# Two value products per block and group, with high and low parts in one stationary tile, and moved start, gate and store work, in a two-layer decoder kernel

## The chip, the cores and the metric

The kernel runs on one core of a Trainium2 chip. A core has TensorE (matrix products; PE in the profile, with PEld for its weight loads), VectorE (DVE), ScalarE (ACT), GpSimd (POOL) and SyncE (SP), which issues most DMAs. Each engine works through its own instructions in order. Products are summed in PSUM banks of 128 partitions by 512 float32 columns. The metric is the device time of one execution in microseconds; lower is better.

## The reference

Two layers of a hybrid decoder trunk, 1024 positions, width 1024, all in float32. Cut to what matters here:

```python
for l in range(DEPTH):
    mod = silu(c) @ ada_w[l] + ada_b[l]            # six shifts, scales, gates
    h = rms_norm(x, g_pre_mix[l]) * (1 + scale_m) + shift_m
    q, k, v, u = split(h @ w_in[l] + b_in[l])      # 8 query heads, 2 key/value heads of 64
    q, k = partial_rotary(q, positions), partial_rotary(k, positions)
    attn = sliding_window_attention_with_sinks(q, k, v, sinks[l])   # window and block 128
    pool = causal_pool_mixer(u, pool_w[l], pool_scale[l])
    mix = concat([attn, pool]) @ w_out[l]
    x = x + gate_m * rms_norm(mix, g_post_mix[l])
    h = rms_norm(x, g_pre_ffn[l]) * (1 + scale_f) + shift_f
    f = (silu(h @ w_gate[l]) * (h @ w_up[l])) @ w_down[l]
    x = x + gate_f * rms_norm(f, g_post_ffn[l])
```

## The kernel before

Every float32 operand of a product is split into a high part (a copy rounded to float32r, on ScalarE) and a low part (the rest, a subtraction on VectorE); `split` does both. A product of two such operands is three products on TensorE, `mm3`: high by high, high by low, low by high.

The 1024 positions are two halves of 512, each four blocks of 128. A layer has a mixing stage and a channel stage. In the mixing stage, `q_pass`, `kv_pass` and `u_pass` multiply by `w_in`, attention and pooling run beside them, and `mix_out` multiplies by `w_out`. The channel stage (`up_firsts`, `up_pair`, `down`) multiplies by `w_gate`, `w_up` and `w_down` with sums of quarters, fewer products than the plain form.

In the mixing stage TensorE's order is the order in which the code issues (`tc.manual_schedule`). `weave` runs a dense chain of products and steps side chains in between: a step that yields a gap is due again once so many units have been issued. A unit, `STEP`, is 12 products of 512 columns. The constants `LEADS` (attention), `GAPS`, `CLOSE`, and the numbers handed to `ada_flow`, `attention` and `pool_mix` are such gaps. On the other engines a scheduler orders by readiness and priority.

Attention runs in groups, one for each block and key/value head `n` (four query heads): 32 groups in all. A group turns keys and queries, forms scores (`att_scores`), exponentials (`att_softmax`), turns the probabilities (`att_probs`), and multiplies by values (`att_values`). Sequence block 0 of each layer has one part of values; each other block has two, `vz` (its own values) and `dz` (the step from the block before), with the probabilities masked for the second. So there are 60 pairs of group and part. The values of the two heads lie in a tile of three fields, with 64 columns of zeros between them that GpSimd writes (`att_vals`, L948); group 0 takes the first two fields and group 1 the last two, so that both sum into one PSUM tile `pv`, each filling half of the partitions with zeros:

```python
vh, vl = (v[:, n : n + 2].rearrange("p a d -> p (a d)") for v in vals)
ins = mm3(pv, vh, vl, *probs, opening, closing, None if opening else attn["open"])
```

The bank opens with group 0 and closes with group 1, and then one ScalarE copy (L1075) takes it to `cat`.

`pv` has one PSUM bank. `part` hands out halves of rings of wide tiles, `raw` (2), `hi` (3) and `lo` (3); weights, keys and queries share `hi`, and weights and pooled values share `lo`. `weight_once` loads a weight tile, splits it, and for some keys stores both parts to DRAM (`parted`), from where the second half reads them back into a whole tile of the ring `lo` (L247): in layer 0 those of `u`, in layer 1 all.

The start: SyncE loads `c`, the rows of biases and norms, and the first columns of `ada_w`; ScalarE's queue loads `x`; VectorE works out the rotary angles. The end: for the last half's tiles, `ended` squares and sums a product tile on ScalarE, multiplies it by the gate row G on VectorE (L1778), and `finish` scales, adds the residual and stores.

Of the kernel before, what the change touches and what calls it, by code (L numbers as in the profile page):

```python
# [68 lines left out]
def hybrid_decoder_kernel(  # L69
# [39 lines left out]
        mix=dict(cfa=2, cfb=2, qkv=5, bqkv=1, uT=4, pt=2, vz=4, dz=2, qT=1, pth=4, pwh=1, pwl=1),  # L109
# [41 lines left out]
    nc.gpsimd.dma_start(pos_i, positions[0].rearrange("(t p) -> p t", p=P))  # L151
# [27 lines left out]
    nc.sync.dma_start(c_raw, c[0].rearrange("(p j) -> p j", j=KD))  # L179
    x0 = []  # L180
    for t in range(NT):
        x0.append(t_("fn", [P, D]))
        nc.scalar.dma_start(x0[t], x[0, t * P : (t + 1) * P, :])
# [10 lines left out]
    def rotary_angles():  # L194
        nc.vector.tensor_copy(pos_f, pos_i)
        for i in range(RH):
            nc.vector.tensor_scalar(ang[:, :, i], pos_f, float(inv_freq[i]), None, op0=ALU.mult)
        nc.vector.tensor_scalar(turns, ang, 1.0 / (2.0 * math.pi), None, op0=ALU.mult)
        nc.vector.tensor_scalar(turns, turns, ROUND_MAGIC, None, op0=ALU.add)
        nc.vector.tensor_scalar(turns, turns, ROUND_MAGIC, None, op0=ALU.subtract)  # L200
# [4 lines left out]
        nc.vector.tensor_scalar(up, ang, math.pi, -math.pi, op0=ALU.min, op1=ALU.max)
        nc.vector.tensor_scalar(sin_t[:, :, halves[0]], up, -1.0, None, op0=ALU.mult)
        nc.vector.tensor_tensor(turns, sin_t[:, :, halves[0]], up, op=ALU.max)
        for half in halves:
            nc.vector.tensor_scalar(cos_t[:, :, half], turns, -1.0, math.pi / 2.0, op0=ALU.mult, op1=ALU.add)
# [320 lines left out]
    def ada_gate(l, sub):  # L530
# [3 lines left out]
        def close(half, hi, lo):  # L534
# [9 lines left out]
            nc.vector.tensor_add(gb, bank[0:1, :], gb)  # L544
# [213 lines left out]
    def finish(h, t, fn, ss, G, xt=None, ahead=None):  # L758
# [6 lines left out]
        for i in range(2):  # L765
# [5 lines left out]
            else:  # L771
                nc.vector.scalar_tensor_tensor(
                    fn[t][:, cs], fn[t][:, cs], rstd, xt[:, cs], op0=ALU.mult, op1=ALU.add
                )
# [290 lines left out]
    def att_values(n, vals, probs, opening, closing, cat, t):  # L1065
# [8 lines left out]
        if closing:
            nc.scalar.activation(  # L1075
# [768 lines left out]
```

## Time and profile before

| what | value |
| --- | --- |
| median of 3 runs | 1867.78 us (1867.1 to 1868.0) |
| the profiled execution | 1870.79 us |
| its span on the core | 1869.1 us |
| granted TensorE clock, mean | 0.997 |
| mean DMA rate over the span | 195 GB/s |

The page gives busy time by engine, then the span in 40 slices of 46.7 us (busy tenths), and the costliest groups:

```profile
PE   7999999999999999999999999999999999999998
DVE  7899885688888978879778788856878888877687
ACT  4885785562222223445648559755522222244452
DMA  9646744665456556844586676446646456574343
```

A group's line names the line of the program, the engine, what is written and read, the count, and after the bar the busy time and the mean of one. An idle time of an engine that is not the bound costs nothing. Start times in a timeline count from the start of the span.

### The profile page before, as it was taken

What the parts mean: (1) busy time and instruction counts of PE and PEld (TensorE: products, weight loads), DVE (VectorE), ACT (ScalarE), POOL (GpSimd) and SP (SyncE); (2) the same over time, 40 slices, a digit from 0 to 9 for tenths busy, and PEclk for the clock granted to TensorE, in tenths of its full rate; (3) what the DMA queues carried; (4) which work ended last, traced back from release to release, by engine and by line L of the source; (5) the groups of instructions that cost most, each with busy time, mean ns of one, the idle gap of its engine ahead of it and who ended that gap; (6) DMA issues with size and microseconds to landing.
All of it is one profiled execution on the core that took longest, in us unless ns stands there. A gap on an engine that the chain in (4) does not pass through costs nothing.

```text
span 1869.1 us, 25361 instructions
## 1 busy us (share of the span) xinstructions
PE 1835.1 (98%) x8662; PEld 1515.4 (81%) x8662; DVE 1501.5 (80%) x2492; ACT 919.7 (49%) x1757; POOL 100.3 (5%) x204
## 2 busy tenths in 40 slices
PE   7999999999999999999999999999999999999998
PEld 5888888888888888888887788888887887888886
DVE  7899885688888978879778788856878888877687
ACT  4885785562222223445648559755522222244452
POOL 0021130000000000000001202200000000000000
PEclk9999999999999999999999999999999999999999
DMA  9646744665456556844586676446646456574343
GB/s 341 201 141 215 259 147 143 208 215 181 167 188 218 183 180 225 298 147 133 194 302 202 213 233 217 155 135 209 220 157 207 162 200 229 176 270 142 113 146 114
DMA packets 237089, 363.84 MB, mean 195 GB/s; under 512 B 17912, under 2 KB 126344, under 8 KB 236960
## 3 DMA queue, kind: packets, MB, share of 16 engines
q1 hardware_dynamic: 236352, 360.13, 57.2%
q10 hardware_dynamic: 576, 2.10, 0.3%
q8 instruction: 68, 1.11, 0.2%
q14 instruction: 61, 0.50, 0.1%
q0 software_dynamic: 32, 0.00, 0.0%
HBM read 274.59 MB, written 87.57 MB: 194 GB/s over the span
## 4 chain that ended last, share of the span: by engine, by line
PE 83%; DVE 8%; DMA 4%; ACT 3%; issue 1%; SPq 1%; DVEq 0%; POOL 0%; ACTq 0%; POOLq 0%
PE acc L285 75%; PE msc L285 3%; PE msc L290 2%; PE pv L285 2%; DVE lo L224 1%; DMA raw<-in_w_up_dram 1%; DMA raw<-in_w_in_dram 1%; ACT hi L223 1%; DVE fn L1322 1%; SPq L426 0%; DVE ada L581 0%; DMA ar<-x 0%; DVE st L1026 0%; ACT sb L1034 0%; DVE raw L1337 0%
## 5 line engine op out<-in xcount | busy, mean ns | idle before, releaser
L223 ACT ACTIVATE hi<-raw 128x1024 fp32r<-128x1024 f32 (+2 forms) x360 | 315.6, 889 | 385.2 <-PE acc L285 243.6
L224 DVE TENSOR_TENSOR lo<-raw,hi 128x1024 fp32r<-128x1024 f32 (+2 forms) x360 | 363.0, 1016 | 115.9 <-ACT hi L223 110.7
L285 PE MATMUL acc<-t,hi 128*128 128x512 f32 x1408 | 432.1, 390 | 3.2 <-ACT hi L223 3.2
L285 PEld LDWEIGHTS acc<-t,hi 128*128 128x128 f32 x1408 | 263.6, 188 | 59.7 <-ACT hi L223 5.6
L285 PE MATMUL acc<-t,lo 128*128 128x512 f32 x704 | 271.9, 389 | 0.8 <-DVE lo L224 0.8
L285 PE MATMUL acc<-hT,hi 128*128 128x512 f32 x832 | 260.2, 394 | 0.0
L285 PE MATMUL acc<-hT,lo 128*128 128x512 f32 x608 | 213.4, 393 | 0.5 <-DVE lo L224 0.4
L285 PE MATMUL acc<-bh,hi 128*128 128x512 f32 x520 | 202.8, 390 | 0.0
L285 PE MATMUL acc<-bh,lo 128*128 128x512 f32 x520 | 202.4, 389 | 0.0
L1322 DVE TENSOR_TENSOR fn<-acc,fn 128x512 f32<-128x512 f32 x220 | 150.8, 686 | 33.7 <-PE acc L285 33.6
L285 PEld LDWEIGHTS acc<-hT,hi 128*128 128x128 f32 x832 | 151.8, 188 | 28.1
L285 PEld LDWEIGHTS acc<-t,lo 128*128 128x128 f32 x704 | 132.1, 188 | 30.0 <-DVE lo L224 2.4
L285 PEld LDWEIGHTS acc<-hT,lo 128*128 128x128 f32 x608 | 112.4, 188 | 25.8 <-DVE lo L224 1.3
L285 PE MATMUL acc<-ph,hi 128*128 128x512 f32 x328 | 126.5, 390 | 0.0
L1247 ACT ACTIVATE fn<-fn 128x512 f32<-128x512 f32 x44 | 27.9, 633 | 188.2 <-DVE fn L1322 188.2
L285 PEld LDWEIGHTS acc<-bh,lo 128*128 128x128 f32 x520 | 97.6, 188 | 20.4
L285 PEld LDWEIGHTS acc<-bh,hi 128*128 128x128 f32 x520 | 97.6, 188 | 20.2
L285 PE MATMUL acc<-b,hi 128*128 128x512 f32 x352 | 108.4, 389 | 0.0
L285 PE MATMUL acc<-lo,hT 128*128 128x512 f32 (+1 forms) x352 | 95.8, 349 | 3.9 <-DMA lo<-parted 2.9
L223 ACT ACTIVATE bh<-two_b 128x512 fp32r<-128x512 f32 x100 | 62.3, 623 | 71.2 <-PE acc L285 70.5
L285 PE MATMUL acc<-hi,hT 128*128 128x512 f32 (+1 forms) x320 | 88.8, 351 | 0.6 <-ACT hT L223 0.5
L285 PE MATMUL acc<-hi 128*128 128x512 f32 x224 | 87.6, 391 | 0.8 <-DVE fn L806 0.8
(320 smaller groups left out, 3235.3 us busy)
## 6 DMA issues: line engine op xcount, KB each, us to landing
raw<-in_w_gate_dram SPq DMA_DIRECT2D x44, 512.0 KB
raw<-in_w_up_dram SPq DMA_DIRECT2D x44, 512.0 KB
cfb<-in_ada_w_dram SPq DMA_DIRECT2D x80, 256.0 KB
raw<-keeps SPq DMA_DIRECT2D x40, 512.0 KB
keeps<-fn SPq DMA_DIRECT2D x66, 256.0 KB
ar<-in_ada_w_dram SPq DMA_DIRECT2D x64, 256.0 KB
two_b<-in_w_down_dram SPq DMA_DIRECT2D x30, 512.0 KB
lo<-parted SPq DMA_DIRECT2D x28, 512.0 KB
```

What stands on the lines that cost most here:

```text
L223: a = nc.scalar.activation(hi, src, AF.Copy)
L224: v = nc.vector.tensor_sub(lo, src, hi.bitcast(F32))
L285: return nc.tensor.matmul(dst, lhs, rhs, start=start, stop=stop)
L290: return nc.tensor.transpose(dst, src, eye_)
L1247: nc.scalar.activation(g, g, AF.Silu)
L1322: nc.vector.tensor_add(halves_of(dst)[m], bank, halves_of(src)[m])
```

## The change

The edits, by place:

- Values: `att_vals` writes one tile with high and low part of each head side by side (64 + 64 columns). `att_values` multiplies it by the high and by the low probabilities, two products. High rows land in partitions 0 to 63 of `pv`, low rows in 64 to 127. Each group opens and closes the bank itself; a ScalarE copy brings the low half to `cat` and a VectorE add puts the high half on top. The tiles `vz` and `dz` are half as many.
- Start: `x` and `c` come over SyncE's queue, ahead of the rows (now in a tile `ada`) and of `ada_w`; positions over ScalarE's. The rotary angles are worked out on GpSimd, the cosines later on VectorE. The first row of `ada_w` products is issued before the turn of the rows.
- `weight_once`: six more tiles (`EARLY`) of layer 0 are stored, over GpSimd's queue, and read back for the second half in place of being loaded and split again. Reads take the rings `lo` and `hi` in turn.
- Gate row: ScalarE copies the bank, and GpSimd adds and multiplies in place of VectorE.
- End: the product with G of the last tiles goes to another tile.
- Gaps: `CLOSE`, `GAPS`, `LEADS` and others have new values.

```diff
-    nc.sync.dma_start(c_raw, c[0].rearrange("(p j) -> p j", j=KD))
-    x0 = []
+    x0 = [t_("fn", [P, D]) for _ in range(NT)]
     for t in range(NT):
-        x0.append(t_("fn", [P, D]))
-        nc.scalar.dma_start(x0[t], x[0, t * P : (t + 1) * P, :])
+        nc.sync.dma_start(x0[t], x[0, t * P : (t + 1) * P, :])
+        if t == 0:
+            nc.sync.dma_start(c_raw, c[0].rearrange("(p j) -> p j", j=KD))
...
     def rotary_angles():
-        nc.vector.tensor_copy(pos_f, pos_i)
+        nc.gpsimd.tensor_copy(pos_f, pos_i)
...
+    acc = ada_first_row(wss[0])
     par = layer_cols(0, rows0)
-    acc = ada_first_row(wss[0])
...
     parted = {}
+    EARLY = ("q4_0", "q5_0", "q6_0", "q7_0", "kv4_0", "kv6_0")
...
         if key in parted:
-            both = part("lo", 1024)
+            recent["ring"] = "hi" if recent.get("ring") == "lo" else "lo"
+            both = part(recent["ring"], 1024)
...
-        if key[0] == "u" or key[-1] == "1":
+        early = key in EARLY
+        if early or key[0] == "u" or key[-1] == "1":
...
-                nc.sync.dma_start(both[:, i * 512 : (i + 1) * 512], src.bitcast(F32))
+                (nc.gpsimd if early else nc.sync).dma_start(both[:, i * 512 : (i + 1) * 512], src.bitcast(F32))
...
-            nc.vector.tensor_add(gb, bank[0:1, :], gb)
-            nc.vector.tensor_mul(gb, gb, gg)
+            gr = t_("ph", [P, 512], F32R)[0:1].bitcast(F32)
+            nc.scalar.activation(gr, bank[0:1, :], AF.Copy)
+            nc.gpsimd.tensor_add(gb, gr, gb)
+            nc.gpsimd.tensor_mul(gb, gb, gg)
...
-        vh = t_(tag, [P, 3, HD], F32R)
-        vl = t_(tag, [P, 3, HD], F32R)
-        for v in (vh, vl):
-            nc.gpsimd.tensor_copy(v[:, 1, :], picks[:, 0:1].bitcast(F32).to_broadcast([P, HD]))
+        both = t_(tag, [P, NKV, 2, HD], F32R)
         vsrc = src.rearrange("p (n d) -> p n d", d=HD)
-        nc.scalar.activation(vh[:, 0:3:2, :], vsrc, AF.Copy)
-        nc.vector.tensor_sub(vl[:, 0:3:2, :], vsrc, vh[:, 0:3:2, :].bitcast(F32))
-        return vh, vl
+        nc.scalar.activation(both[:, :, 0, :], vsrc, AF.Copy)
+        nc.vector.tensor_sub(both[:, :, 1, :], vsrc, both[:, :, 0, :].bitcast(F32))
+        return both
...
-        vh, vl = (v[:, n : n + 2].rearrange("p a d -> p (a d)") for v in vals)
-        ins = mm3(pv, vh, vl, *probs, opening, closing, None if opening else attn["open"])
-        if opening:
-            attn["open"] = ins
+        both = vals[:, n].rearrange("p o d -> p (o d)")
+        mm(pv, both, probs[0], opening, False)
+        mm(pv, both, probs[1], False, closing)
         if closing:
-            nc.scalar.activation(
-                cat[:, :, t * P : (t + 1) * P], pv.rearrange("p (j q) -> p j q", j=GRP), AF.Copy
-            )
+            high, low = (pv[o * HD : (o + 1) * HD].rearrange("p (j q) -> p j q", j=GRP) for o in range(2))
+            dst = cat[n * HD : (n + 1) * HD, :, t * P : (t + 1) * P]
+            nc.scalar.activation(dst, low, AF.Copy)
+            nc.vector.tensor_add(dst, high, dst)
...
-                att_values(n, vals, prob, n + i == 0, n == NKV - 1 and i == len(parts) - 1, cat, t)
+                att_values(n, vals, prob, i == 0, i == len(parts) - 1, cat, t)
...
-    LEADS = (0.9, 0.85, 0.21, 2.72, 1.2, 0.94)
+    LEADS = (0.9, 0.9, 0.25, 2.72, 1.2, 0.75)
...
-                nc.vector.tensor_mul(fn[1][t][:, 0:512], fn[1][t][:, 0:512], G[:, 0:512])
-                finish(1, t, fn[1], ss[1], G, tail[t], aheads[t])
+                nc.vector.tensor_mul(fn[0][t][:, 0:512], fn[1][t][:, 0:512], G[:, 0:512])
+                finish(1, t, (fn[0][t], fn[1][t]), ss[1], G, tail[t], aheads[t])
```

TensorE's order in the first half's attention, at the second block's first group (its second value part, `pv<-pth,dz`) and the second group's first part (`pv<-pth,vz`); `acc` are products of `q_pass` and `u_pass`, `msc<-sa,qT` scores. Before:

```order
L285 MATMUL pv<-pth,dz 128x512 x3
L285 MATMUL msc<-sa,qT 128x256 x4
L285 MATMUL acc<-hi,hT 128x512
L285 MATMUL acc<-lo,hT 128x512
L285 MATMUL acc<-hi,hT 128x512
L285 MATMUL msc<-sa,qT 128x256 x4
L285 MATMUL acc<-hi,hT 128x512
L285 MATMUL acc<-lo,hT 128x512
L285 MATMUL acc<-hi,hT 128x512 x2
L285 MATMUL acc<-lo,hT 128x512
L285 MATMUL acc<-hi,hT 128x512
L285 MATMUL pv<-pth,vz 128x512 x3
```

And of the change:

```order
L292 MATMUL pv<-pth,dz 128x512 x2
L292 MATMUL acc<-hi,hT 128x512
L292 MATMUL acc<-lo,hT 128x512
L292 MATMUL acc<-hi,hT 128x512
L292 MATMUL msc<-sa,qT 128x256 x4
L292 MATMUL acc<-lo,hT 128x512 x3
L292 MATMUL pv<-pth,vz 128x512 x2
```

The value steps have two products in place of three, and one of the two score steps has moved ahead of the first of them.

SyncE's order in layer 1, while the second half's parted weights are read (`lo<-parted`, `hi<-parted`), between loads of `ada_w` (`cfb`) and the gate's rows (`ar`, `gate`). Before:

```order
L247 DMA lo<-parted 128x1024 x2
L546 DMA gate<-ar 1x512
L539 DMA ar<-in_ada_b_dram 1x512
L247 DMA lo<-parted 128x1024
L568 DMA cfb<-in_ada_w_dram 128x512 x5
L247 DMA lo<-parted 128x1024
```

And of the change:

```order
L253 DMA hi<-parted 128x1024
L253 DMA lo<-parted 128x1024
L577 DMA cfb<-in_ada_w_dram 128x512 x2
L555 DMA gate<-ar 1x512
L577 DMA cfb<-in_ada_w_dram 128x512 x2
L253 DMA hi<-parted 128x1024
L253 DMA lo<-parted 128x1024
```

The reads go to two rings in turn, and the store of the gate row stands between loads of `ada_w`.

ScalarE's order at the start: splits of weights (`hi<-raw`), the row of `ada_w` (`ar<-msc`), the first normalised pieces (`uT<-msc`) and their split (`hT<-uT`). Before:

```order
L223 ACTIVATE hi<-raw 128x512 x2
L450 ACTIVATE ar<-msc 1x256
L223 ACTIVATE hi<-raw 128x512
L667 ACTIVATE uT<-msc,colp 128x512
L223 ACTIVATE hT<-uT 128x512
```

And of the change:

```order
L227 ACTIVATE hi<-raw 128x512 x2
L457 ACTIVATE ar<-msc 1x256
L676 ACTIVATE uT<-msc,colp 128x512
L227 ACTIVATE hi<-raw 128x512
L227 ACTIVATE hT<-uT 128x512
```

The piece `uT` has moved ahead of the third split of a weight.

More of the change, by code (lines that the diff above doesn't have):

```diff
@@ L108, in hybrid_decoder_kernel @@
     REGIONS = dict(
-        mix=dict(cfa=2, cfb=2, qkv=5, bqkv=1, uT=4, pt=2, vz=4, dz=2, qT=1, pth=4, pwh=1, pwl=1),
+        mix=dict(cfa=2, cfb=2, qkv=5, bqkv=1, uT=4, pt=2, vz=2, dz=1, qT=1, pth=4, pwh=1, pwl=1),
         up=dict(t2=8, t1=8, t3=8, b22=8, t4=8),
@@ L150, in hybrid_decoder_kernel @@
     pos_i = const.tile([P, NB], I32, name="pos_i")
-    nc.gpsimd.dma_start(pos_i, positions[0].rearrange("(t p) -> p t", p=P))
+    nc.scalar.dma_start(pos_i, positions[0].rearrange("(t p) -> p t", p=P))
     ones_r = const.tile([P, 1], F32R, name="ones_r")
@@ L194, in rotary_angles @@
     def rotary_angles():
-        nc.vector.tensor_copy(pos_f, pos_i)
+        nc.gpsimd.tensor_copy(pos_f, pos_i)
         for i in range(RH):
[L197 to L200, printed above, removed]
+            nc.gpsimd.tensor_scalar(ang[:, :, i], pos_f, float(inv_freq[i]), None, op0=ALU.mult)
+        nc.gpsimd.tensor_scalar(turns, ang, 1.0 / (2.0 * math.pi), None, op0=ALU.mult)
+        nc.gpsimd.tensor_scalar(turns, turns, ROUND_MAGIC, None, op0=ALU.add)
+        nc.gpsimd.tensor_scalar(turns, turns, ROUND_MAGIC, None, op0=ALU.subtract)
         for part in two_pi_parts():
-            nc.vector.scalar_tensor_tensor(ang, turns, -part, ang, op0=ALU.mult, op1=ALU.add)
+            nc.gpsimd.tensor_scalar(cos_t[:, :, 0:RH], turns, -part, None, op0=ALU.mult)
+            nc.gpsimd.tensor_add(ang, cos_t[:, :, 0:RH], ang)
         halves = [slice(0, RH), slice(RH, ROT)]
         up = sin_t[:, :, halves[1]]
[L205 to L209, printed above, removed]
+        nc.gpsimd.tensor_scalar(up, ang, math.pi, -math.pi, op0=ALU.min, op1=ALU.max)
+        nc.gpsimd.tensor_scalar(sin_t[:, :, halves[0]], up, -1.0, None, op0=ALU.mult)
         for g, w in enumerate(WINDOWS):
@@ L212, in rotary_angles, with rotary_cosines @@
         nc.vector.reciprocal(rcnt, rcnt)
+    def rotary_cosines():
+        halves = [sin_t[:, :, 0:RH], sin_t[:, :, RH:ROT]]
+        after(nc.vector.tensor_tensor(turns, *halves, op=ALU.max), recent["split"])
+        for half in (slice(0, RH), slice(RH, ROT)):
+            nc.vector.tensor_scalar(cos_t[:, :, half], turns, -1.0, math.pi / 2.0, op0=ALU.mult, op1=ALU.add)
     def rotary_tables(prev):
@@ L387, in hybrid_decoder_kernel, with load_col_rows @@
     NROW = 6 * KD + 2 * KD + 4 + 4
-    def load_col_rows(l):
-        rows = t_("ar", [P, 512])[:NROW, :P]
+    def load_col_rows(l, tag="ar"):
+        rows = t_(tag, [P, 512])[:NROW, :P]
         r = 0
@@ L772, in finish @@
                 nc.vector.scalar_tensor_tensor(
-                    fn[t][:, cs], fn[t][:, cs], rstd, xt[:, cs], op0=ALU.mult, op1=ALU.add
+                    fn[1][:, cs], fn[i][:, cs], rstd, xt[:, cs], op0=ALU.mult, op1=ALU.add
                 )
-            nc.sync.dma_start(out[0, h * T + rows.start : h * T + rows.stop, cs], fn[t][:, cs])
+            nc.sync.dma_start(out[0, h * T + rows.start : h * T + rows.stop, cs], (fn[t] if xt is None else fn[1])[:, cs])
     def natural_proj(fn, left, wsrc, ss, G, last, free):
@@ L1167, in pool_mix @@
             late = (g, hi, lo_)
-            yield 1.7 if h else 2.82
+            yield 2.37 if h else 2.81
         mapped(*late)
@@ L1639, in gate_flow @@
             one, two = ada_gate(l, 0)
-            yield from ada_flow([one], [cats[0][1][:, i, :] for i in range(4)], 2.25)
+            yield from ada_flow([one], [cats[0][1][:, i, :] for i in range(4)], 2.39)
             while 1 not in cats:
                 yield 0.5
-            yield from ada_flow([two], [cats[1][1][:, i, :] for i in range(4)], 1.91)
+            yield from ada_flow([two], [cats[1][1][:, i, :] for i in range(4)], 2.49)
         gate = Chain(gate_flow())
-        att = attention(0, qkvs[0], par["sink"], cats[0][0], 0.47, 3.23)
+        att = attention(0, qkvs[0], par["sink"], cats[0][0], 0.55, 3.23)
         def dense():
@@ L1660, in hybrid_decoder_kernel @@
         late = att
-        att = attention(1, qkvs[1], par["sink"], cats[1][0], 14.0, 3.95)
+        att = attention(1, qkvs[1], par["sink"], cats[1][0], 11.6, 3.95)
         ring = [cats[1][1][:, i, :] for i in range(4)]
-        pair = Chain(ada_flow(ada_pair(l, 1, par["cols"], par["abf"]), ring, 0.91))
+        pair = Chain(ada_flow(ada_pair(l, 1, par["cols"], par["abf"]), ring, 0.77))
         weave(out0, late, att, pair)
```

12 lines of the change are left out of this document (7 added, 5 removed).

## The prediction

> **What bounds the kernel now.** First the page: busy time by engine, then the chain that ended last.
>
> ```profile
> PE 1835.1 (98%) x8662; PEld 1515.4 (81%) x8662; DVE 1501.5 (80%) x2492; ACT 919.7 (49%) x1757; POOL 100.3 (5%) x204
> PE 83%; DVE 8%; DMA 4%; ACT 3%; issue 1%; SPq 1%; DVEq 0%; POOL 0%; ACTq 0%; POOLq 0%
> ```
>
> TensorE is busy for 98% of the span and 83% of the chain lies on it. So a product that disappears is worth its issue time, unless the engine then waits. The issue time is not the mean of 390 ns in the groups (that is start to end, and neighbours overlap); it is read from an unbroken piece of the chain, and the value products show the same pace (three, then the next instruction):
>
> ```profile
> 515.85 85.11 PE acc L285 x375
> 116.22 0.84 PE L285 MATMUL pv<-pth,vz 128*128 128x512 f32 x3
> 116.90 0.39 PE L285 MATMUL acc<-hi,hT 128*128 128x512 f32 x1
> ```
>
> 85.11 / 375 = 0.227 us for one product of 512 columns, and 116.90 - 116.22 = 0.68 us for three. Next, where TensorE waits (microseconds in total, times, longest):
>
> ```profile
> PE msc L402 <- DVE ident L156: 11.8, 1, 11.8
> PE acc L285 <- ACT hi L223: 3.2, 4, 1.4
> PE acc L285 <- DMA lo<-parted: 2.9, 2, 1.6
> PE msc L285 <- ACT qT L999: 2.5, 3, 0.9
> ```
>
> One wait at the start, and small ones. The kernel is bound by TensorE, with a head, a tail and a few short waits around it.
>
> **Values: 60 products less.** The product count and the eviction of before:
>
> ```profile
> L285 PE MATMUL pv<-pth,vz x96: 387/389/632, 86.3 to 1213.4; 128*128 128x512 f32 x96
> L285 PE MATMUL pv<-pth,dz x84: 387/389/478, 112.4 to 1216.8; 128*128 128x512 f32 x84
> L1075 ACT ACTIVATE cfa<-pv x8: 578/582/642, 97.7 to 1079.7; 128x512 f32<-128x512 f32 x8
> L224 DVE TENSOR_TENSOR pth<-msc,pth x32: 671/680/692, 84.4 to 1211.0; 128x512 fp32r<-128x512 f32 x32
> ```
>
> 96 + 84 = 180 products, three for each of 60 (block, group) pairs; two stay, so 60 go: 60 x 0.227 = **-13.6 us**. Weight loads overlap (PEld is its own row), so the wider stationary tile costs nothing.
>
> What is added: each of the 32 head groups gets its own eviction, a ScalarE copy of one half and a VectorE add of the other, where 16 ScalarE copies did before. A 64-partition form is not in the trace; the nearest rows are 0.582 us (PSUM copy of 512 columns) and 0.680 us (PSUM operand, 512 columns), bounds 0 and those. I take the whole 0.58 and 0.68. That is +9.3 us of ScalarE (16 more) and +21.8 us of VectorE, beside TensorE as long as those engines have room:
>
> ```profile
> 60.00:160.00 100.00, 98.00 (x573) 83.36 (x572) 92.42 (x207) 77.14 (x201) 25.81 (x44) 1.00 0.54 173
> 160.00:320.00 160.00, 159.25 (x790) 131.33 (x789) 126.82 (x245) 114.78 (x269) 22.92 (x43) 1.00 0.59 198
> 100.00:120.00 20.00, 20.00 (x112) 16.71 (x111) 19.71 (x45) 16.47 (x46) 5.83 (x9) 1.00 0.48 150
> 120.00:140.00 20.00, 18.97 (x107) 15.94 (x106) 19.76 (x44) 16.05 (x45) 5.91 (x11) 1.00 0.46 145
> L544 DVE TENSOR_TENSOR ar<-msc,ar x8: 666/671/673, 107.0 to 1550.7; 1x512 f32<-1x512 f32 x8
> ```
>
> Columns: stretch, length, then busy PE, PEld, DVE, ACT, POOL. Layer 0's first attention half (60 to 160) is the tight one: VectorE 92.4 of 100 us, and 39.5 of 40 between 100 and 140. There it gains 8 adds (+5.4), and loses four gate operations of 0.67 (-2.7, now on ScalarE and GpSimd) and, as the second half reads ready-made high and low parts of six weight tiles, six splits of 0.68 (-4.1). Net -1.4, but not in the same microseconds: **+1.0 us** (0 to +3.2, the 14 products that this half saves).
>
> **A new wait: the pv bank.** It is one bank. Before, both groups of a block added into it; now the second group opens it afresh and must wait for copy and add of the first. The tightest place is the second block's first group closing and its second opening, whose rows of TensorE's order stand in the part on the change.
>
> Now six products of 512 and four of 256 columns stand between the two value steps; four of 256 columns pass in 1037.54 - 1037.07 = 0.47 us (below), so that is 6 x 0.227 + 0.47 = 1.83 us. In the third block the same count gives 2.55 us, elsewhere 3.9 to 13. What an eviction takes to finish is seen at a late one of before:
>
> ```profile
> 1034.85 0.84 PE L285 MATMUL pv<-pth,dz 128*128 128x512 f32 x3
> 1037.32 0.58 ACT L1075 ACTIVATE cfa<-pv 128x512 f32<-128x512 f32 x1
> 1037.07 0.63 PE L285 MATMUL msc<-sa,qT 128*128 128x256 f32 x4
> 1037.54 0.60 PE L290 MATMUL msc<-ident,sb 128*128 128x128 f32 x4
> ```
>
> It ended 1037.90 - 1035.69 = 2.2 us after the product; without a queue it is 0.6. With the add, 1.4 to 2.9 us, plus 0.16 of the product's own tail. The wait is 0 to 1.3 us at the first place and 0 to 0.6 at the second, for each layer; TensorE runs in order, so everything behind waits too. I take 0.8 a layer: **+1.6 us** (0 to +3.8).
>
> **Reads of ready-made parts.** In layer 1 the second half's weights come back from DRAM:
>
> ```profile
> 1037.89 3.02 PE L285 MATMUL acc<-lo,hT 128*128 128x512 f32 x12
> 1042.23 0.98 PE L285 MATMUL acc<-lo,hT 128*128 128x512 f32 x3 [1.32 <-DMA lo<-parted]
> 1044.78 1.65 PE L285 MATMUL acc<-lo,hT 128*128 128x512 f32 x3 [1.57 <-DMA lo<-parted]
> 1040.94 0.34 SPq L247 DMA_DIRECT2D lo<-parted  x1
> SPq L247 <- PE acc L285: 14.1, 4, 7.6
> 1044.00:1051.00 7.00, 6.22 (x20) 5.07 (x21) 2.23 (x6) 3.56 (x8) 0.00 (x0) 0.51 0.46 131
> ```
>
> The read is issued at 1040.94, just as TensorE's twelve products end: its buffer of the ring lo came free only then. Two waits, 2.9 us, and then 7 us at a granted clock of 0.51 in place of 1.00: 7 x 0.49 = 3.4 us more.
>
> In SyncE's order of now (the part on the change has its rows) the rings hi and lo take turns, so a read has about twice the time to land. It still stands behind loads that wait for VectorE. I take **-5.0 us** of the 6.3 (0 to -6.3).
>
> The stores behind those parts: six of layer 0's tiles are now written out too, by twelve DMAs on GpSimd's queue.
>
> ```profile
> 1.35 1.04 POOL L151 DMA_DIRECT2D pos_i<-in_positions_dram  x1 [0.34 <-issue]
> ```
>
> That is 12 x 1.04 = 12.5 us of GpSimd, which is busy 25.8 of the 100 us from 60 on (and the padding copies of the values go), so I cost it at nothing; were GpSimd's masks late by one store, 1.04 us each.
>
> The Trainium skill (TensorE: Matmul & The Clock Gate, "What's actually happening") lets the clock fall to half only after an idle window of about 3.4 us. The trace disagrees: waits of 1.32 and 1.57 us with products between were followed by 0.51. By the rule the half clock would have another cause, the waits' going would bring back 2.9 at most, and with 2.3 of it in place of 5.0 the sum would be 2.7 less.
>
> **Tail.**
>
> ```profile
> 1859.81 1.42 DVE L772 SCALAR_TENSOR_TENSOR sb<-sb,rs,hT 128x512 f32<-128x512 f32 x2
> 1860.11 0.39 PE L285 MATMUL acc<-two_b,lo 128*128 128x512 f32 x1
> 1861.14 0.68 DVE L1417 TENSOR_TENSOR sb<-acc,sb 128x512 f32<-128x512 f32 x1
> 1862.67 0.69 DVE L1778 TENSOR_TENSOR sb<-sb,G 128x512 f32<-128x512 f32 x1 [0.85 <-ACT junk L614]
> 1863.28 0.15 DVE L750 SCALAR_TENSOR_TENSOR rs<-ss,st 128x1 f32<-128x1 f32 x1
> ```
>
> The gate product L1778 writes over what ScalarE is squaring and waits for it; into another tile it runs beside the squaring. Its 1863.28 - 1862.67 = 0.6 us leaves the last chain; the chain of the tile before it shortens alike, so L1417 starts at the last product's end (1860.50) and not at 1861.14. **-1.2 us** (-0.6 to -1.3).
>
> **Head.**
>
> ```profile
> 0.80 6.51 ACTq L183 DMA_DIRECT2D fn<-in_x_dram  x4
> 12.14 5.86 PE L448 MATMUL msc<-cfa,c_act 128*1 128x256 f32 x16
> 18.12 8.42 DMA raw<-in_w_in_dram
> 26.56 0.30 ACT hi L223
> 27.10 0.77 ACT uT L667
> 28.58 3.09 PE acc L285 x12
> ```
>
> The rotary angles leave VectorE for GpSimd, so the identity and the 11.8 us wait go. x now stands ahead of the weights on SyncE and no longer takes ScalarE 6.51 us to issue; the row of L448 can start when its first weights are there, 10 to 12 us by the 6.51 us and the weights' own issues behind it, in place of 12.14. But what is late next is a weight load that lands at 26.54 whatever TensorE did, and ScalarE's split of it ahead of the hT that frees 28.58. ScalarE's new order (its rows stand in the part on the change) puts uT, 0.77 us, before that split. One more table load on ScalarE stands ahead of the first x, where it has nothing else to do. So not 2 us but **-1.2 us** (0 to -2.5). The moved leads I set at 0 (+2.5 to -2.5, the size of the qT wait).
>
> **Sum.** -13.6 + 1.0 + 1.6 - 5.0 - 1.2 - 1.2 = -18.4. The profiled execution took 1870.8 us (span 1869.1 and 1.7 around it), so it would be 1852.4; it lies 3.0 above the median of 1867.8, which gives **1849.4 us**.
>
> **Rivals.**
> 1. *The reads stay late* (0.20). Six tiles of layer 0 now come as 512 KB and not 256 KB; SyncE issues in order, so the wait of layer 1 may stay or appear in layer 0 too. Against it: two rings. Price 2.9 + 3.4 = 6.3: 1855.7.
> 2. *All waits go* (0.10): no pv wait, the whole 6.3, the qT waits of 2.5 too: 1849.4 - 1.6 - 1.0 - 1.3 - 2.5 = 1843.0.
> 3. *The products were cover* (0.08): TensorE waits for evictions in place of computing, and the 13.6 are lost: 1863.0. It speaks for it that VectorE is at 98.7% from 100 to 140; against it that this holds in 40 us only.
> 4. *VectorE becomes the bound of the mixing stages* (0.04), slower: its net work there (+21.8, less 8 gate operations 5.4 and splits 4.1: +12.3) comes onto the path, and only head and tail gain: 1867.8 + 12.3 - 2.4 = 1877.7. It decides once VectorE is full over a whole stage; the rows say 92% and 79%.
> 5. *The half clock is not the waits'* (0.03): then only waits go, 2.3 of the 2.9, and the time is 1849.4 + 2.7 = 1852.1.
>
> **How the numbers follow.** Forecast 0.55 (own range 1845 to 1854). The range 1841 to 1859 takes in rivals 1, 2 and 5 and the bounds of the unknown waits, and leaves out rivals 3 and 4 and some 0.05 below. A measurement tells about 0.2% (3.7 us) from no change: faster 0.55 + 0.20 + 0.10 + 0.03 of rival 5 + 0.03 of rival 3 = 0.91, same 0.05, slower 0.04.
>
> **What would show it.** Right: 120 value products; TensorE's wait list without lo<-parted and with a pv wait on the new add below 4 us in all; granted clock 1.00 all through both mixing stages; the last product some 7.4 us before the end of the span and not 8.6. Wrong: a long list of pv waits, VectorE without gaps from 60 to 160, a second stretch of half clock, or a first 512-column product later than before.

## The result, and the profile after

| | changed kernel | before, same batch |
| --- | --- | --- |
| median | 1890.2 us (1888.9 to 1891.6, 4 runs) | 1867.9 us (1867.1 to 1868.6, 4 runs) |
| ratio | 1.0119, 95% interval 1.0103 to 1.0135 | |
| span of the profiled execution | 1889.8 us | 1869.1 us |
| granted clock, mean | 0.995 | 0.997 |

The change made the kernel slower by 22 us, where 18.4 us less were forecast. The page of the changed kernel, busy time by engine:

```profile
PE 1831.2 (97%) x8602; PEld 1504.6 (80%) x8602; DVE 1507.5 (80%) x2481; ACT 934.5 (49%) x1776; POOL 120.6 (6%) x199
```

60 products are gone (8662 before), and TensorE's busy share fell from 98 to 97% of a longer span: it issues less and waits more. Three of its waits now (us in total, times, longest), and below them a row of the kernel before that the prediction did not show:

```profile
PE msc L455 <- DMA cfa<-in_ada_w_dram: 11.6, 1, 11.6
PE acc L292 <- DVE lo L228: 10.6, 7, 2.5
PE pv L292 <- DVE cfa L1083: 2.7, 1, 2.7
```

```profile
PE acc L285 <- DVE lo L224: 2.2, 4, 1.0
```

Lines of the changed kernel lie four to nine further down (L228 is L224, L292 is L285, L815 is L806). The list no longer has lo<-parted, as forecast, but waits for split weights (`lo`) rose from 2.2 to 10.6 us. Where they lie, the stretches show (stretch, length, then busy PE, PEld, DVE, ACT, POOL, granted clock, DMA share, GB/s); first before, then the changed kernel:

```profile
480.00:640.00 160.00, 159.33 (x701) 130.41 (x700) 140.23 (x182) 43.04 (x50) 0.00 (x0) 1.00 0.57 200
1060.00:1240.00 180.00, 179.23 (x923) 149.14 (x922) 142.95 (x278) 124.92 (x300) 29.08 (x54) 1.00 0.60 196
```

```profile
60.00:160.00 100.00, 94.62 (x553) 79.19 (x552) 90.51 (x200) 77.17 (x198) 21.19 (x35) 1.00 0.55 185
160.00:320.00 160.00, 155.03 (x766) 126.37 (x765) 132.89 (x260) 117.01 (x275) 21.05 (x33) 1.00 0.61 204
480.00:640.00 160.00, 154.82 (x671) 125.86 (x671) 133.43 (x172) 41.90 (x49) 6.71 (x4) 0.99 0.52 178
1060.00:1240.00 180.00, 173.49 (x905) 143.45 (x905) 152.36 (x303) 131.09 (x317) 31.77 (x45) 0.99 0.61 198
```

TensorE is idle 5.4, 5.0, 5.2 and 6.5 us there, against 2.0, 0.8, 0.7 and 0.8 before. Two things are to be seen. From 480 to 640 lies the channel stage, which has no attention and no values: all that the change touched there is the gate row, and VectorE is emptier than before (133 against 140 us) while TensorE waits for it. And in the first attention half (60 to 160) TensorE waits although VectorE, at 90.5 of 100, is no fuller than before (92.4); in the two other mixing stretches VectorE is busier (132.9 against 126.8 us, 152.4 against 143.0), but not full.

The tail did what was forecast: the last product ends at 1882.4, 7.4 us before the end of the span.

```profile
1881.98 0.39 PE L292 MATMUL acc<-two_b,lo 128*128 128x512 f32 x1
1882.41 0.69 DVE L1423 TENSOR_TENSOR sb<-acc,sb 128x512 f32<-128x512 f32 x1
1883.13 0.69 DVE L1786 TENSOR_TENSOR fn<-sb,G 128x512 f32<-128x512 f32 x1
```

L1423 starts as the last product ends, and the gate product L1786 no longer stands behind ScalarE's squaring.

### The profile page after: what moved, and what is told of

It is laid out like the page before. It is cut to its first block, busy times and chain, and to the rows that moved or that the text cites. A ratio compares the mean times of both kernels' runs of the same rounds, so it can differ in the third digit from the quotient of the medians.

```text
span 1889.8 us, 25275 instructions
## 1 busy us (share of the span) xinstructions
PE 1831.2 (97%) x8602; PEld 1504.6 (80%) x8602; DVE 1507.5 (80%) x2481; ACT 934.5 (49%) x1776; POOL 120.6 (6%) x199
## 4 chain that ended last, share of the span: by engine, by line
PE 67%; DVE 15%; DMA 8%; ACT 6%; issue 3%; SPq 0%; POOL 0%; DVEq 0%; POOLq 0%; ACTq 0%
PE acc L292 61%; PE msc L292 3%; DVE lo L228 2%; DMA raw<-in_w_up_dram 2%; PE msc L297 2%; ACT hi L227 1%; DVE fn L1328 1%; DVE ada L590 1%; DMA raw<-in_w_in_dram 1%; DMA ar<-x 1%; DMA cfb<-in_ada_w_dram 1%; PE pv L292 1%; ACT sb L1040 1%; DVE raw L1343 1%; DVE raw L1344 1%
## 5 line engine op out<-in xcount | busy, mean ns | idle before, releaser
L227 ACT ACTIVATE hi<-raw 128x1024 fp32r<-128x1024 f32 (+2 forms) x354 | 311.3, 892 | 388.2 <-PE acc L292 217.8
L228 DVE TENSOR_TENSOR lo<-raw,hi 128x1024 fp32r<-128x1024 f32 (+2 forms) x354 | 359.6, 1022 | 120.8 <-ACT hi L227 114.4
L292 PE MATMUL acc<-t,hi 128*128 128x512 f32 x1408 | 434.1, 391 | 4.5 <-ACT hi L227 4.4
L292 PEld LDWEIGHTS acc<-t,hi 128*128 128x128 f32 x1408 | 264.9, 189 | 62.6 <-ACT hi L227 8.0
L292 PE MATMUL acc<-hT,hi 128*128 128x512 f32 x928 | 287.3, 395 | 0.0
L292 PE MATMUL acc<-t,lo 128*128 128x512 f32 x704 | 273.4, 392 | 9.6 <-DVE lo L228 9.6
L292 PE MATMUL acc<-bh,hi 128*128 128x512 f32 x520 | 202.9, 390 | 1.2 <-ACT sb L1426 1.2
L292 PE MATMUL acc<-bh,lo 128*128 128x512 f32 x520 | 202.4, 389 | 0.0
L292 PEld LDWEIGHTS acc<-hT,hi 128*128 128x128 f32 x928 | 168.7, 188 | 31.0
L292 PE MATMUL acc<-hT,lo 128*128 128x512 f32 x512 | 188.7, 392 | 1.0 <-DVE lo L228 1.0
L292 PEld LDWEIGHTS acc<-t,lo 128*128 128x128 f32 x704 | 132.8, 189 | 40.4 <-DVE lo L228 13.0
L292 PE MATMUL acc<-ph,hi 128*128 128x512 f32 x328 | 126.5, 390 | 0.0
L292 PEld LDWEIGHTS acc<-bh,hi 128*128 128x128 f32 x520 | 97.6, 188 | 21.8 <-ACT sb L1426 1.7
L292 PEld LDWEIGHTS acc<-bh,lo 128*128 128x128 f32 x520 | 97.6, 188 | 20.5
L292 PEld LDWEIGHTS acc<-hT,lo 128*128 128x128 f32 x512 | 95.4, 188 | 21.8 <-DVE lo L228 1.8
L292 PE MATMUL acc<-b,hi 128*128 128x512 f32 x352 | 108.4, 389 | 0.0
L292 PE MATMUL acc<-hi,hT 128*128 128x512 f32 (+1 forms) x400 | 102.4, 350 | 1.1 <-ACT hT L227 0.7
L292 PE MATMUL acc<-hi 128*128 128x512 f32 x224 | 89.0, 397 | 6.6 <-DVE fn L815 5.5
L292 PE MATMUL acc<-lo,hi 128*128 128x512 f32 x224 | 87.8, 392 | 0.0
```

Source lines behind the costliest of these rows:

```text
L227: a = nc.scalar.activation(hi, src, AF.Copy)
L228: v = nc.vector.tensor_sub(lo, src, hi.bitcast(F32))
L292: return nc.tensor.matmul(dst, lhs, rhs, start=start, stop=stop)
```

## The experiments

All were timed in three rounds against the kernel before. "Difference" is the ratio less one, times 1868 us.

| run | ratio (95% interval) | difference, us |
| --- | --- | --- |
| e1 changed kernel, gate row on VectorE | 1.0019 (1.0005 to 1.0033) | +3.5 |
| e2 before + two value products | 1.0104 (1.0087 to 1.0121) | +19.4 |
| e3 before + gate row on ScalarE, GpSimd | 1.0101 (1.0086 to 1.0116) | +18.9 |
| e4 changed kernel, gaps of before | 1.0195 (1.0177 to 1.0213) | +36.4 |
| e5 changed kernel, values of before | 1.0105 (1.0082 to 1.0128) | +19.6 |
| e6 e1, values of before | 1.0032 (1.0018 to 1.0045) | +6.0 |
| e7 e1, without the VectorE adds | 0.9973 (0.9958 to 0.9988) | -5.0 |
| e9 e1, without the early stores | 1.0030 (1.0017 to 1.0044) | +5.6 |
| e10 before + start, stores, reads, end | 1.0043 (1.0027 to 1.0058) | +8.0 |
| e12 before + new gaps | 1.0047 (1.0032 to 1.0063) | +8.8 |
| e13 before + ScalarE copy, gate row on VectorE | 1.0015 (1.0005 to 1.0024) | +2.8 |
| e14 e2, without the VectorE adds | 1.0049 (1.0031 to 1.0068) | +9.2 |
| e15 e10, without the early stores | 0.9992 (0.9982 to 1.0002) | -1.5 |
| e16 before + reads and end | 0.9999 (0.9987 to 1.0011) | -0.2 |
| e17 before + three gaps moved by a hair | 1.0033 (1.0019 to 1.0048) | +6.2 |
| e18 e14, third product put back | 1.0011 (1.0001 to 1.0021) | +2.1 |
| e19 e3, row stored by GpSimd | 1.0118 (1.0099 to 1.0138) | +22.0 |
| e20 e1, third product put back | 1.0052 (1.0033 to 1.0072) | +9.7 |

### The gate row

The theory after the result: the gate row, not the values, holds up the channel stage. Undone in the changed kernel (e1), done alone in the kernel before (e3):

```diff
-            gr = t_("ph", [P, 512], F32R)[0:1].bitcast(F32)
-            nc.scalar.activation(gr, bank[0:1, :], AF.Copy)
-            nc.gpsimd.tensor_add(gb, gr, gb)
-            nc.gpsimd.tensor_mul(gb, gb, gg)
+            nc.vector.tensor_add(gb, bank[0:1, :], gb)
+            nc.vector.tensor_mul(gb, gb, gg)
```

> The changed kernel with one part undone: VectorE adds and multiplies the gate row again, straight from the bank. Theory G (the gate row on GpSimd is what costs: SyncE's queue waits 3.2 us for it ahead of the weight loads of the channel stage, and the channel stages of the changed kernel wait some 18 us more on TensorE than before): 1872 us, between 1862 and 1875. Theory V (the values' new bank wait and evictions cost it) or theory P (the new gaps): 1886 to 1891.

> The kernel before with the gate row on ScalarE and GpSimd alone. Theory G: 1868 + 18 = 1886 us, between 1880 and 1892, with TensorE waits in the channel stages as in the changed kernel. Theories V and P: 1866 to 1870.

Both came out as theory G had it. Undoing it takes 18.7 us off (22.2 less 3.5), doing it alone adds 18.9, and in the changed kernel with the values of before it costs 13.6 (e5 less e6, below): one edit makes up most of the result, whichever kernel it stands in. How it does so, SyncE's queue shows, from the row's first product (`picks`) on. Before:

```profile
515.22 0.40 PE L542 MATMUL msc<-ph,picks 128*1 128x512 f32 x1
517.16 0.50 SPq L1305 DMA_DIRECT2D raw<-in_w_up_dram  x1
519.63 0.25 SPq L546 DMA_DIRECT2D gate<-ar  x1
```

The changed kernel, at the same place:

```profile
519.91 0.40 PE L549 MATMUL msc<-ph,picks 128*1 128x512 f32 x1
521.24 2.41 POOL L553 TENSOR_TENSOR ar<-ph,ar 1x512 f32<-1x512 f32 x1 [227.44 <-ACT ph L552]
523.74 1.27 POOL L554 TENSOR_TENSOR ar<-ar 1x512 f32<-1x512 f32 x1
525.04 0.24 SPq L555 DMA_DIRECT2D gate<-ar  x1
525.76 0.42 SPq L1311 DMA_DIRECT2D raw<-in_w_up_dram  x1
543.10 0.73 PE L292 MATMUL acc<-t,lo 128*128 128x512 f32 x1 [1.88 <-DVE lo L228]
```

Two things have moved. SyncE's order now has the row's store ahead of the load of `w_up`, where it stood behind; and the store waits for GpSimd. So the load of `w_up` is issued 525.76 - 519.91 = 5.9 us after the row's product and not 517.16 - 515.22 = 1.9. 17 us later TensorE waits 1.88 us for the low part of a weight. The eight row halves on each engine, in the changed kernel on GpSimd, and before on VectorE (the product; its sum L544 took 671 ns):

```profile
L553 POOL TENSOR_TENSOR ar<-ph,ar x8: 1327/2074/2912, 109.9 to 1567.0; 1x512 f32<-1x512 f32 x8
L554 POOL TENSOR_TENSOR ar<-ar x8: 1267/1284/1622, 112.8 to 1570.0; 1x512 f32<-1x512 f32 x8
```

```profile
L545 DVE TENSOR_TENSOR ar<-ar x8: 648/669/671, 108.3 to 1551.9; 1x512 f32<-1x512 f32 x8
```

Is it the extra hop over ScalarE, or GpSimd? e13 has the hop and leaves the arithmetic on VectorE (`nc.vector.tensor_add(gb, gr, gb)`):

> The kernel before, with the gate row copied by ScalarE first and then added and multiplied on VectorE as before: the extra hop without GpSimd. If GpSimd's slow add and multiply (2.07 and 1.28 us against 0.67 and 0.65) are the cause of the gate row's cost: near before, 1867 to 1872, ratio 0.999 to 1.001. If a hop and a later end of the row by some 0.6 us is enough to make the loads behind it late: 1880 to 1889, ratio 1.006 to 1.010.

At 1873.0 us it lies just above the range for GpSimd as the cause and far below the other. The hop adds 2.8 us (0.9 to 4.5), so some 16 of the 18.9 are GpSimd's. In its trace the load stands ahead of the store again, at the old distance:

```profile
516.95 0.50 SPq L1307 DMA_DIRECT2D raw<-in_w_up_dram  x1
519.44 0.25 SPq L548 DMA_DIRECT2D gate<-ar  x1
```

If the store in SyncE's queue is the cause, it helps to issue it elsewhere (e19: `nc.gpsimd.dma_start(row[:, o], gb)`):

> The kernel before with the gate row on ScalarE and GpSimd (1888.6 before, +18.6), but the row's store issued by GpSimd behind its own product and not by SyncE, so that SyncE's loads of w_gate and w_up no longer stand behind a store that waits for GpSimd. If SyncE's queue behind that store is the cause: the waits at 540, 657, 1448 and 1565 go (11.6 us), and with GpSimd's hold on VectorE in the mixing stages left, 1873 to 1879, ratio 1.002 to 1.005. If the cause is GpSimd's hold on VectorE, or the row's buffers coming free late: 1884 to 1889, ratio 1.008 to 1.010.

It did not help (+22.0). The expectation was wrong, and the queue of e19 shows why the run does not clear GpSimd either:

```profile
521.71 1.28 POOL L547 TENSOR_TENSOR ar<-ar 1x512 f32<-1x512 f32 x1
523.01 0.33 SPq L376 DMA_DIRECT2D ar<-in_ada_w_dram  x1
523.39 0.44 SPq L1307 DMA_DIRECT2D raw<-in_w_up_dram  x1
```

With the store gone, the next load into the ring `ar`, whose buffer the row occupies until GpSimd's product ends, stands at the same place in the same queue and waits just as long. The load of `w_up` is 523.39 - 517.88 = 5.5 us behind the row's product (at 517.88) as against 5.9. By these traces the load is late behind whatever in SyncE's order waits for GpSimd ahead of it. A version in which nothing of the kind stands there was not tried, so that this lateness is the whole price is not shown. The wait between is VectorE's: its sums of weight pairs (L1337 before, L1339 in the runs) need the loads, and the low parts that TensorE then waits for come out of them. How long those sums waited for the channel stage's loads, in all and how often, in e13, then in e3, then in e19 (before: 13.7, 8 times):

```profile
  DVE raw L1339: 11.4, 10
```

```profile
  DVE raw L1339: 17.5, 11
```

```profile
  DVE raw L1339: 33.3, 16
```

The runs with the row on GpSimd are the ones that wait longest, but these waits do not add up to the price: from the kernel before to e3 they grow by 3.8 us, and e19 waits nearly twice as long as e3 for 3 us more. In TensorE's own list of e3 the waits for `lo` are 5.9 us longer than before (2.2), and those for parted weights, loads of the same queue, 3.1 longer (2.9):

```profile
PE acc L285 <- DVE lo L224: 8.1, 7, 2.3
PE acc L285 <- DMA lo<-parted: 6.0, 3, 3.2
```

The profiled execution of e3 spans 1886.9 us, 17.8 more than before. Of these, 11.5 are idle time of TensorE (45.5 against 34.0), and 6.3 are busy time for the same 8662 products (1841.4 against 1835.1), at a mean granted clock of 0.993 against 0.997: a wait cost its own length and, in some places, slower products behind it.

### The values: were the products cover?

Two products for three, and nothing else (e2), with the gaps of before; then the same without the 32 adds (e14), whose output lacks the products with the values' high parts:

```diff
             nc.scalar.activation(dst, low, AF.Copy)
-            nc.vector.tensor_add(dst, high, dst)
```

> The kernel before with the values' two products alone. Theory G: the 60 products come out as forecast, less a bank wait: 1856 us, between 1853 and 1860. Theory V: no faster than before, 1866 or more.

> The kernel before with two value products and gaps of before, but without the 32 VectorE adds (the output lacks the products with the values' high parts). With the adds it took 1889.3. If VectorE's fullness by the adds is what costs the 20 us: 1855 to 1868, ratio 0.992 to 1.000. If the loss is that the gaps of before leave the attention chains too few products of cover, whoever evicts: 1878 to 1889, ratio 1.005 to 1.010. In between, about 1881, the adds cost what they cost with the new gaps (7.6 us).

Alone, the values cost 19.4 us where 11 were to be won. The adds, with the waits for the bank that hang on them, are about half of it (19.4 less 9.2); e14's 1877.4 us lies next to the range in which the gaps leave too little cover. The rest is there without them: 60 products gone and the time 9.2 longer. So e18 puts the third product back into e14 (the low probabilities' product issued twice; the output counts it twice and lacks the high rows):

```diff
         mm(pv, both, probs[0], opening, False)
+        mm(pv, both, probs[1], False, False)
         mm(pv, both, probs[1], False, closing)
```

> The run of two products with the gaps of before and without the VectorE adds (1877.4), with the third product put back in its place (the low probabilities' product issued twice, so the output counts it twice, and lacks the high rows): the products of before, with the evictions of each group on ScalarE. If the removed products were cover, and their going is what brought the waits: the waits fall back and the time is that of before, 1867 to 1872. If the bank's two evictions and their waits are the cause: 1877.4 + 13.6 = 1891.

13.6 us more work make it 7.1 us faster (9.2 less 2.1). The stretches show where the waits come and go, e14 first, then e18:

```profile
60.00:160.00 100.00, 95.89 (x561) 80.85 (x560) 91.56 (x203) 79.59 (x204) 18.26 (x32) 1.00 0.54 172
160.00:320.00 160.00, 154.56 (x755) 125.43 (x754) 124.35 (x245) 117.86 (x273) 19.60 (x30) 0.99 0.60 196
1060.00:1240.00 180.00, 174.09 (x902) 143.21 (x901) 142.09 (x281) 126.62 (x300) 22.41 (x38) 1.00 0.61 197
```

```profile
60.00:160.00 100.00, 97.31 (x570) 82.78 (x569) 91.88 (x206) 78.97 (x203) 19.90 (x32) 1.00 0.54 172
160.00:320.00 160.00, 158.87 (x786) 130.56 (x786) 126.78 (x246) 118.37 (x274) 17.34 (x30) 1.00 0.60 198
1060.00:1240.00 180.00, 178.41 (x926) 148.55 (x925) 144.01 (x282) 128.76 (x307) 20.71 (x36) 1.00 0.62 198
```

TensorE's idle time in these 440 us falls from 4.1 + 5.4 + 5.9 = 15.4 us to 2.7 + 1.1 + 1.6 = 5.4, with VectorE and ScalarE about as busy (within 2.5 us in each stretch). With the gaps of before the products acted as cover: with them gone the waits are there, with them back they mostly are not. That they covered the length of chains on ScalarE and VectorE, at whose links TensorE now arrives early, is the reading that fits engines that are not full; it was not tested by itself. The 7.1 us are no more than what the order alone can move (6.2 in e17, below); it is the place of the idle time that speaks for cover. That 16 more ScalarE copies and a bank opened by each group cost 2.1 us (0.2 to 3.9) is the rest of e18.

The new gaps were in the change as well, so e7 and e20 ask the same in the changed kernel with the gate row on VectorE (e1): e7 leaves the adds out (output as in e14), e20 puts the third product back.

> The changed kernel with the gate row on VectorE and without the VectorE add that puts the high half on top (the output lacks the products of the values' high parts). Theory V with the cost in VectorE's 32 adds of 0.67 us: 1855 to 1862. Theory V with the cost in the wait for the bank or in ScalarE's 16 copies more: 1868 to 1873, little better than with the add.

> The changed kernel with the gate row on VectorE (1873.4), with the third product put back (the low probabilities' product issued twice, so the output counts it twice). If with the new gaps the 60 products' going does pay: 1873.4 + 13.6 = 1887, ratio 1.009. If they were cover there too, as with the gaps of before (where putting them back cost nothing): 1870 to 1876, ratio 1.000 to 1.003.

The adds cost 8.5 us there too, and e7's 1865.8 us lies between its two ranges. The 60 products do pay with the new gaps, but 6.2 us (9.7 less 3.5) of their 13.6: between the two theories. Idle time of TensorE from 60 to 320 shows the rest, in e1:

```profile
60.00:160.00 100.00, 95.38 (x556) 79.61 (x554) 91.56 (x204) 76.70 (x197) 21.99 (x31) 1.00 0.60 194
160.00:320.00 160.00, 156.67 (x764) 127.51 (x765) 129.89 (x256) 117.10 (x273) 19.81 (x32) 0.99 0.60 195
```

It is 8.0 us, against 2.8 in the kernel before.

### Gaps, start, stores, reads

e4 gives the changed kernel the gaps of before; e5 and e6 give it and e1 the values of before; e9 takes the early stores (`EARLY = ()`) from e1.

> The changed kernel with the gaps (CLOSE, GAPS, LEADS and those handed to the flows) of before. Theory P (the new gaps put TensorE in wait): 1880 us or less. Theories G and V: 1886 to 1892.

> The changed kernel with the values as before (three products, padded tiles, one eviction for each block). Theory V (copy and add of each group cost about 20 us of waits on TensorE, more than the 13.6 us of products, whatever the gaps are): the gate row's 17 us stay and the values' loss of some 6 goes, 1878 to 1886. Theory W (the new gaps were made for the two products and fit the three badly, as the old gaps fit the two badly): 1893 or more.

> The same with the gate row back on VectorE as well, so that start, stores, rings, end and new gaps are left. Theory V: faster than before, 1860 to 1867. Theory W: 1872 or more.

> The changed kernel with the gate row on VectorE and without the six early stores (loads and splits as before). Theory V: within 3 us of 1873.4, on either side, since what is gained in splits is lost in reads. If the twelve stores on GpSimd's queue or the wider reads are what costs: 1866 or less.

The new gaps are worth 14.2 us in the changed kernel (36.4 less 22.2). With the gate row on VectorE the values show a gain of 2.5 us (6.0 less 3.5), with it on GpSimd a loss of 2.6 (22.2 less 19.6); the intervals overlap in both cases, so neither can be told from nothing. Of the four expectations, e4 missed both its ranges (1905.6 us) and e5 (1889.7) lies between its two; e6 (1876.9) came out as theory W had it, and e9 (1876.4) within the 3 us. The early stores gain 2.1 with the new gaps, within the intervals. e6 leaves a puzzle: start, stores, reads, end and gaps together are 6.0 slower than before, where 7.4 were to be won. So each alone in the kernel before:

> The kernel before with only the start, the early stores and reads on both rings, and the tail's gate tile changed; values, gate row and gaps as before. If the three edits are worth what the prediction gave them (reads -5.0, tail -1.2, head -1.2): 1868 - 7.4 = 1862.6, ratio 0.996. If only the tail pays and the stores' traffic takes the rest: 1867 to 1869, ratio 0.999 to 1.000. If the sum of the four edits measured so far is additive (the changed kernel with old gaps 1905.6, less 20 for the values and 17 to 18.6 for the gate row): 1867 to 1868.6. If the +6.5 of the run with new gaps and old values lies in these three edits and not in the gaps: 1876, ratio 1.003.

> The kernel before with only the gaps of the changed kernel. If the gaps are made for two products and cost where three are issued: 1874 to 1878, ratio 1.003 to 1.005. If gaps matter only through the values' evictions: 1867 to 1871, ratio 0.999 to 1.001. If they are better in themselves: 1860 or less, ratio 0.995.

> The run with start, stores and end (1878.1 against 1869.0 of before, +9.1) without its six early stores: start, reads on both rings in layer 1, and the tail's gate tile remain, with values, gate row and gaps as before. If the early stores and their reads in layer 0 cost the 9 us (a read that TensorE waited for at 130, with half clock behind it): 1860 to 1863, ratio 0.996, since the reads of layer 1 lost their wait and half clock (-5) and the tail gained 1.2. If the start's other order costs it, by moving everything behind it: 1874 to 1879, ratio 1.003 to 1.005.

> The kernel before with two edits alone: reads take both rings in turn (layer 1 alone has many), and the tail's gate product goes to another tile. By the prediction's own terms for them (-5.0 and -1.2): 1862.8, ratio 0.9967. If only the tail is kept, since another wait takes the place of the reads': 1867 to 1868, ratio 0.999. If any shift of the ring's order costs elsewhere: 1870 or more.

The new gaps without the two products cost 8.8, and start, stores, reads and end with the old gaps 8.0; together they cost 6.0 (e6), so these prices do not add. With the gaps of before, the early stores cost 9.5 (e10 less e15): a read that came back late in layer 0, the place that rival 1 named. e10's row, and the stretch behind it at a granted clock of 0.59:

```profile
129.62 0.98 PE L292 MATMUL acc<-lo,hT 128*128 128x512 f32 x3 [1.76 <-DMA lo<-parted]
```

```profile
130.00:134.20 4.20, 4.20 (x18) 3.37 (x17) 3.04 (x8) 1.11 (x5) 0.06 (x1) 0.59 0.50 134
```

That wait and half clock are some 3.5 us of the 9.5 (an estimate: 1.76 + 4.2 x 0.41); the rest is not traced. e15's 1869.4 us is in neither of its ranges. Start, reads and end without the stores are no gain that can be told (-1.5), nor are reads and end alone (-0.2), although both waits that they were to remove are gone from e16's trace: no lo<-parted, and its last product at 1858.4 lies 7.3 us before the end of the span (1865.7). The place of the reads, before and in e16:

```profile
960.00:1060.00 100.00, 94.66 (x532) 79.61 (x532) 76.51 (x172) 66.43 (x171) 16.91 (x36) 0.97 0.70 228
```

```profile
960.00:1060.00 100.00, 97.28 (x556) 81.72 (x555) 79.17 (x179) 69.06 (x181) 18.13 (x38) 1.00 0.76 254
```

TensorE's idle time falls from 5.3 to 2.7 us and the granted clock rises from 0.97 to 1.00, which over 100 us is some 3 us more (an estimate).

How much of such differences is the order alone? e17 moves three gaps of the kernel before by a hair:

```diff
-    LEADS = (0.9, 0.85, 0.21, 2.72, 1.2, 0.94)
+    LEADS = (0.9, 0.9, 0.25, 2.72, 1.2, 0.94)
...
-        att = attention(0, qkvs[0], par["sink"], cats[0][0], 0.47, 3.23)
+        att = attention(0, qkvs[0], par["sink"], cats[0][0], 0.55, 3.23)
```

> The kernel before with three of the gaps moved by a hair (attention's begin 0.47 to 0.55, two of its leads 0.85 to 0.9 and 0.21 to 0.25; a unit is 12 products), and nothing else: what the order alone is worth. If the time depends little on the order, as the prediction's 0 (-2.5 to +2.5) has it: 1866 to 1871, ratio 0.9985 to 1.0013. If the order of before stands on a narrow point, so that any shift costs 4 to 10 us: 1873 to 1879, ratio 1.002 to 1.005.

No product, copy or load was added or removed, and the time is 6.2 us longer (3.5 to 9.0). No run that computes the whole reference was faster than the kernel before by more than its interval.

## Why the prediction was wrong

In the order of its terms, and with what each measured. Taken apart along e6, e1 and the changed kernel, the 22.2 us are +6.0 (start, stores, reads, end, gaps), -2.5 (values) and +18.7 (gate row); forecast were -7.4, -11.0 and no price of its own. So of the 40.6 us between forecast (-18.4) and measurement (+22.2), the gate row is 18.7; the other 21.9 are forecast gains that did not come, and losses in their place: 13.4 in the first group and 8.5 in the values.

- **The gate row: the step that failed.** The prediction counted it only as relief: VectorE "loses four gate operations of 0.67 (-2.7, now on ScalarE and GpSimd)". It never asked how long they take on GpSimd or who stands behind their end. It measured +18.7 and +18.9 (e1, e3), and 13.6 between e5 and e6. GpSimd takes 2.07 and 1.28 us where VectorE took 0.67 each; SyncE's queue turns that into a weight load 4 us later, and TensorE into waits of up to 2.5 us. That GpSimd and not the hop makes it is shown (e13); that the load's lateness is the path by the traces of three kernels, though the run made to take the wait away (e19) put another in its place.
- **Values, 60 x 0.227.** The products went, and their price was right as issue time. The rival "the products were cover", given 0.08 because VectorE is full in 40 us only, was largely right, on other grounds: in e14 and e18 VectorE is equally busy, and the waits come and go with the products. The products paid 6.2 with the new gaps, and with the old ones cost 7.1 when removed (e20, e18).
- **The adds and the bank, +2.6.** The durations were right: 0.594 us for the copy of 64 partitions and 0.68 for the add. With their waits the adds cost 8.5 on the path (e7), 10 with the gaps of before. The bank wait measured 2.7 us, one wait on the add L1083 where 0 to 3.8 were allowed. The bound that was too low was that of the adds beside other work, +3.2.
- **Parted reads, -5.0.** The wait went as forecast in the changed kernel and e16 (e1 has one of 2.1 us again, on `hi<-parted`); the gain did not come: e16 has reads and end at -0.2 (-2.4 to +2.1) for a forecast of -6.2. The two rows of that place, under e16, show some 5 to 6 us won there; but elsewhere waits came, such as one of 1.7 us for `hi` (L988), which the list of the kernel before lacks. Part may also be that the profiled execution lay 3 us above the median, and the waits were read from it; that is argued, not shown.
- **Tail, -1.2.** Right: 8.6 us became 7.4.
- **Head, -1.2.** Too much: the first wait is 11.6 us in place of 11.8, now for the first weights of `ada_w`, but the first 512-column product came at 23.26 in place of 23.11: the head gained nothing. That later product is one of the signs that the prediction listed against itself.
- **Early stores, nothing.** -2.1 with the new gaps, +9.5 with the old ones.
- **Moved leads, 0 (-2.5 to +2.5).** The bound was taken from the waits for qT. Three small moves alone are +6.2, all the new gaps +8.8 in the kernel before and -14.2 in the changed one: the largest unknown of the change stood at nothing, with bounds of 2.5 either way.

## What to carry to other kernels

When work is moved to another engine, price it there, and then read what the in-order queues that wait for its end have behind them: here some 2 us more in each of eight short rows became 18.7 us, and the traces show weight loads that stand behind the row's end. A product that TensorE no longer issues is worth its issue time only where no chain was paced by it; put it back without its purpose, as e18 does, and see whether the time moves. Where the order is tuned by constants, move them by a hair first: that spread (6 us here) is the bound of every small term.

## What was unexpected of the hardware

**VectorE beside GpSimd.** In the changed kernel's mixing stage short VectorE operations are stretched while GpSimd works on the row:

```profile
109.89 1.54 POOL L553 TENSOR_TENSOR ar<-ph,ar 1x512 f32<-1x512 f32 x1
110.22 1.25 DVE L1033 TENSOR_SCALAR st<-st 128x4 f32<-128x4 f32 x1
112.75 1.51 POOL L554 TENSOR_TENSOR ar<-ar 1x512 f32<-1x512 f32 x1
113.06 1.38 DVE L949 TENSOR_TENSOR qkv<-qkv,cos_t 128x160 f32<-128x160 f32 x1
```

L1033 takes 161 ns and L949 323 ns in the median of their groups; each is some 1.1 us longer here and ends at or near the end of GpSimd's operation. Over the whole of e3 such stretches are small: its VectorE instructions add up to 1628.5 us against 1636.4 before, and the 16 that left had taken 10.7, so the others grew by some 2.8 us in all (an estimate). What they cost on the path was not measured.

**GpSimd's price.** The Trainium skill (GPSIMD Engine Reference, "Elementwise — side-by-side cycle accounting") gives a two-input float32 add of 2048 columns on GpSimd 1.96 times VectorE's time. The changed kernel's trace agrees for the product of the row, 1284 against 669 ns, and not for its add, 2074 ns in the median. In e3 the same add has a median of 1364:

```profile
L546 POOL TENSOR_TENSOR ar<-ph,ar x8: 1279/1364/2913, 109.2 to 1562.7; 1x512 f32<-1x512 f32 x8
```

Its four adds in the mixing stages take 1.28 to 1.29 us there, 1.9 times VectorE's 0.67, and three of the four in the channel stages 2.41 to 2.91, as all four do in the changed kernel. Ahead of those GpSimd had stood idle for over 100 us, but the fourth in e3, also after such a rest, took 1.44. Why the others are longer was not tested.

**Half clock.** After the wait for the bank in layer 1's attention the clock fell, where the prediction had 1.00 all through both mixing stages (the wait, and the stretch behind it):

```profile
1050.78 0.73 PE L292 MATMUL pv<-pth,vz 128*128 128x512 f32 x2 [2.69 <-DVE cfa L1083]
```

```profile
1051.00:1055.50 4.50, 4.50 (x16) 3.58 (x16) 4.47 (x11) 1.51 (x6) 0.00 (x0) 0.62 0.77 241
```

A wait of 2.69 us here, and of 1.76 in e10, was followed by a stretch of about 0.6. The Trainium skill (TensorE: Matmul & The Clock Gate, "What's actually happening") asks for an idle window of about 3.4 us; in this kernel shorter waits were enough. Their length does not decide it alone: in the changed kernel waits of 1.88 us (up to 543.1) and 2.49 us (up to 659.6) were followed by a mean clock of 0.76 and 0.78 over the next 7 us, and waits of 2.83 us (up to 182.8) and 2.49 us (up to 1476.4) by 1.00.
